# A hybrid encoder layer on one core: transfers and reciprocals of the attention mix dealt over later steps, five dense parts at the head of the out-projection, norm sums by head pair

## The chip, the cores and the metric

The kernel runs on one core of a Trainium2 chip. The core has four engines that compute: TensorE (PE, matrix products; its weight loads are shown as PEld), VectorE (DVE), ScalarE (ACT) and GpSimd (POOL); SyncE (SP) only issues transfers. Each engine runs its own instructions in order and waits for the others by semaphores. What counts is the device time in microseconds (us), the median of several runs.

## The reference, cut to what matters

One layer of an encoder, for 1024 positions of width 1024, in float32. Two mixers stand side by side: mixer A is dense attention (8 query heads on 2 key heads), mixer B a mixture of three dilated windows (8 heads). Their outputs are normed apart, go through one out-projection and are added to x; then follows a gated channel mixer of width 2816 with a convolution over three positions.

```
hn = rms_norm(x, norm1_g)
proj = hn @ w_in                       # 1024 x 2304: qA kA vA qB kB vB
out_a = global_gqa_attention(qa, ka, va)
out_b = dilated_mixture_attention(rms_norm(qb), rms_norm(kb), vb)
mixed = concat([rms_norm(out_a, outa_norm_g), rms_norm(out_b, outb_norm_g)])
x = x + mixed @ w_out
x = x + conv_ffn(rms_norm(x, norm2_g), w_up, conv_w, conv_b, w_down)
```

## The kernel before

Each float32 operand is split into a high and a low half (an ACT copy for the high, a DVE subtraction for the low), and each product is three matmuls: high by high, high by low, low by high. That is why most values pass ACT and DVE ("split") before PE may use them.

The stages follow one another on PE: some warm-up products of constants (`WARM`, L595), the projection with its norms (to some 188 us), mixer A in 16 groups (`a_main_bounded`, to 331), mixer B in 36 steps of which four make a head (`dilated`, to 458), the out-projection (`project`, to some 571), the up-projection with the convolution (`product`, to 975) and the down-projection. A scheduler of the framework orders the instructions of each engine from the order of the program and the waits. `with tc.issue_after(x)` keeps what is written under it behind instruction x on its engine: in this text, it is pinned behind x.

Both mixers make their outputs transposed, heads on partitions and positions in columns, with the softmax denominators as one more row. To divide by them, the row is written out by a transfer, comes back as a small tile, is inverted, is written out again (`rna` for A, `rnb` for B) and is read back spread over the 64 partitions of a head. For mixer A these are `recip_load` (L800), `recip` (L803, L804), `scale_load` (L811) and the multiplication `scale_a` (L814); `squares` (L817, L818) and `squares_sum` (L823, a small matmul with ones) then make the sums for the output norm. For mixer B, at the end of a head, two ACT copies (L1052, L1053) take the head's result out of PSUM, the denominators go out (L1055), `b_move` (L1060) moves the head into place, `b_recip` holds the reciprocal (L1064), the write (L1065) and the spread (L1066), and `scale_b` multiplies a pair of heads (L1070).

In mixer B a step is: scores on PE (`b_s_bounded`, L1014), exponentials on ACT (L1015), multiplication by the distance weights on DVE (`b_p_bounded`: L1023 in the coarse steps, L1027, L1029, L1030 in the fine ones) and, three steps later, the products with the values on PE (`b_pv_bounded`, L1042, L1049). Scores and results lie in PSUM banks that are used in turn, so PE's scores wait for the DVE multiplication of an earlier step. The table `dilated_late` puts the late work of mixer A into steps of mixer B, `dense_late` into groups of mixer A. The fills (L1274) write constants into tiles for mixer B.

The out-projection works in 16 parts: (i, 0) is the half of tile i (128 positions) that comes from mixer A, called dense here, (i, 1) that from mixer B. A part is two halves of 12 matmuls (`part_out`, L1187 to L1189) over six PSUM banks. `mix_split` (L1200, L1201) splits a part's input, `part_add` (L1195) scales its output by the norm and adds x (`x_part`, L1204, loads it) or the first half. Behind (i, 1) `h2_a` makes the second norm (squares L1223, tiny operations of DVE, L1233) and writes the tile out (L1234, `rscr`); `h2_b` transposes it on PE (L206) and splits it (L229 to L256), and `t_split` (L1263, L1264) and `wu_prep` (L1646 to L1656) make the sums that the up-projection takes.

All loads and stores of these stages are issued by SP, in one order. The lines that set the steps of mixer B are

```
h1, i1 = divmod(n - 8, 4)
if h1 >= 0 and i1 == 0:
    b_recip(h1)
```

so that head h's reciprocal is written in step 4h + 8 and its `b_move` in step 4h + 7; the last head's stand in `project()`, where `b_move(7)` is called once more.

Of the kernel before, what the change touches and what calls it, by code (L numbers as in the profile page):

```python
# [20 lines left out]
D = 1024  # L21
# [50 lines left out]
WARM = 10  # L72
# [22 lines left out]
F_ACS = (O_F + 6048, O_F + 6048, O_F + 2048)  # L95
# [20 lines left out]
F_XS = [O_F + o for o in (2560, 7680, 0, 1024)]  # L116
# [28 lines left out]
def tile_encoder_layer(ctx, tc, x, xT, w_in, w_kv, consts, norm2_g, w_out, w_up, convs,  # L145
# [17 lines left out]
    def emit(bounded):  # L163
# [578 lines left out]
        pairs = [1]  # L742

        def a_main_bounded(g, prep, tail, late, plan, late_plan):
# [23 lines left out]
            for j in range(4):  # L768
# [9 lines left out]
                act(f(p, 1024), bank(st, 1024), AF.Exp)  # L778
# [4 lines left out]
                vec.tensor_tensor(r(pl, 1024), f(p, 1024), rf(ph, 1024), op=OP.subtract)  # L783
# [36 lines left out]
        def squares_sum(ns, where, dst):  # L820
            b = next_tr()
            for c, n in enumerate(ns):
                mm(bank(b, 1, c), f(F_ACS[where] + 128 * (n % 2), 128), f(O_ONE, 1), start=True, stop=True)  # L823
            if where == 2:
                vec.tensor_scalar(f(dst + ns[0], len(ns)), bank(b, len(ns)), 1.0 / 512, EPS, op0=OP.mult, op1=OP.add)
            else:
                act(f(dst + ns[0], len(ns)), bank(b, len(ns)), AF.Copy, scale=1.0 / 512, bias=EPS)
# [189 lines left out]
        exps, probs = {}, [None]  # L1017
# [14 lines left out]
        def b_pv_bounded(h, i):  # L1032
# [18 lines left out]
            if i == 3:  # L1051
                act(f(F_OS, 512)[0:65], bank(6)[0:65], AF.Copy)  # L1052
                act(f(F_OS + 512, 512)[0:65], bank(7)[0:65], AF.Copy)  # L1053
# [8 lines left out]
        def b_recip(h):  # L1062
# [3 lines left out]
            dma(rf(R_RBB[h // 2 % 2], 1024)[p:p + 64], spread_row(None, rnb[h], 1024))  # L1066
# [108 lines left out]
        parts = [(0, 0), (1, 0), (2, 0), (3, 0), (0, 1), (1, 1), (4, 0), (2, 1), (5, 0), (3, 1), (6, 0), (4, 1), (7, 0), (5, 1), (6, 1), (7, 1)]  # L1175
# [15 lines left out]
        def part_add(i, u):  # L1191
            x0, o = F_XS[i % 4], (F_XS[i % 4], qab(seq(i)))[u]
            scale = f((SM_A + 16 + seq(i), SM_B + i)[u], 1)
            for hf in range(2):
                vec.scalar_tensor_tensor(f(o + 512 * hf, 512), bank(part_bank(i, u, hf)), scale, f(x0 + 512 * hf, 512),  # L1195
                                         op0=OP.mult, op1=OP.add)
# [6 lines left out]
        def x_part(i):  # L1203
            dma(f(F_XS[i % 4], 1024), perm_rows(x, seq(i), D))  # L1204

        def scale_out(i, n):
            v, rt, t = [f(SM_T + o + i, n) for o in (32, 40, 72)]
            act(rt, v, AF.Sqrt)
            newton(f(SM_B + i, n), v, rt, t)

        def hn(i):
            return F_X if i == 7 else F_HN

        def h2_a(i):
            t = SM_T + 48 + 8 * (i % 2)
            o = qab(seq(i))
            if bounded:
                part_add(i, 1)
# [904 lines left out]
```

## Time and profile before

| | |
|---|---|
| median of three runs | 1197.47 us (1195.58 to 1198.71) |
| profiled execution | 1197.74 us |
| its span, first to last instruction | 1196.0 us |
| mean granted clock of PE | 0.994 |
| DVE busy, 478 to 572 us | 77.9 of 94 us |
| DMA, share of 16 engines, 458 to 478 us | 0.74 |

The times of an execution are a little longer than its span, since starting and ending lie outside it. The profile gives busy times by engine and by group of instructions, for each wait the engine or transfer that ended it, and the clock that TensorE was granted (1.00 is full speed).

### The profile page before, as it was taken

What the parts mean: (1) busy time and instruction counts of PE and PEld (TensorE: products, weight loads), DVE (VectorE), ACT (ScalarE), POOL (GpSimd) and SP (SyncE); (2) the same over time, 40 slices, a digit from 0 to 9 for tenths busy, and PEclk for the clock granted to TensorE, in tenths of its full rate; (3) what the DMA queues carried; (4) which work ended last, traced back from release to release, by engine and by line L of the source; (5) the groups of instructions that cost most, each with busy time, mean ns of one, the idle gap of its engine ahead of it and who ended that gap; (6) DMA issues with size and microseconds to landing.
All of it is one profiled execution on the core that took longest, in us unless ns stands there. A gap on an engine that the chain in (4) does not pass through costs nothing.

```text
span 1196.0 us, 16295 instructions
## 1 busy us (share of the span) xinstructions
PE 1169.5 (98%) x5736; PEld 961.7 (80%) x5736; DVE 1018.8 (85%) x1402; ACT 659.5 (55%) x975; POOL 332.0 (28%) x238
## 2 busy tenths in 40 slices
PE   9999998999998998999999999999999999999998
PEld 8888886666678997787788888888888888888886
DVE  7869888899986885878999999999999997966673
ACT  6875737799886872636444453444444363543331
POOL 0000222510033420012465565645566413000000
PEclk9999999999998999999999999999999999999999
DMA  8556320121037777222223232332323267967962
GB/s 317 163 151 163 84 70 10 32 71 52 23 78 165 171 198 206 91 87 97 80 80 107 97 115 97 109 112 98 115 79 115 105 203 272 339 225 249 297 225 75
DMA packets 137783, 162.11 MB, mean 136 GB/s; under 512 B 55712, under 2 KB 91744, under 8 KB 137568
## 3 DMA queue, kind: packets, MB, share of 16 engines
q1 hardware_dynamic: 135552, 155.26, 41.4%
q0 software_dynamic: 2144, 5.77, 2.2%
q8 instruction: 46, 0.75, 0.3%
q14 instruction: 41, 0.34, 0.1%
HBM read 117.86 MB, written 33.91 MB: 127 GB/s over the span
## 4 chain that ended last, share of the span: by engine, by line
PE 77%; DVE 7%; DMA 6%; ACT 4%; issue 3%; POOL 2%; SPq 1%; DVEq 0%; POOLq 0%; ACTq 0%
PE ps L1689 11%; PE ps L1687 11%; PE ps L1688 11%; PE ps L1829 6%; PE ps L1830 6%; PE ps L1831 6%; PE ps L757 6%; PE ps L450 2%; PE ps L449 2%; PE ps L451 2%; PE ps L772 2%; PE ps L773 2%; PE ps L1187 2%; PE ps L1189 2%; PE ps L1188 1%
## 5 line engine op out<-in xcount | busy, mean ns | idle before, releaser
L1687 PE MATMUL ps<-bigr 128*128 128x512 f32 x616 | 240.0, 390 | 0.6 <-ACT bigr L1263 0.5
L1689 PE MATMUL ps<-bigr 128*128 128x512 f32 x616 | 239.9, 389 | 0.5 <-DVE bigr L1656 0.5
L1688 PE MATMUL ps<-bigr 128*128 128x512 f32 x616 | 239.8, 389 | 0.0
L1726 DVE SCALAR_TENSOR_TENSOR bigf<-bigf 128x768 f32<-128x768 f32 (+1 forms) x176 | 194.0, 1138 | 1.5 <-ACT bigf L1721 0.8
L1655 ACT ACTIVATE bigr<-bigf 128x512 fp32r<-128x512 f32 x154 | 92.0, 623 | 148.4 <-POOL bigf L1647 112.5
L1809 ACT ACTIVATE bigr<-bigf 128x1024 fp32r<-128x1024 f32 (+1 forms) x99 | 84.0, 869 | 115.2 <-PE ps L1831 66.6
L1687 PEld LDWEIGHTS ps<-bigr 128*128 128x128 f32 x616 | 115.6, 188 | 25.9 <-ACT bigr L1263 1.0
L1689 PEld LDWEIGHTS ps<-bigr 128*128 128x128 f32 x616 | 115.6, 188 | 24.8 <-DVE bigr L1656 0.9
L1688 PEld LDWEIGHTS ps<-bigr 128*128 128x128 f32 x616 | 115.6, 188 | 24.0
L1829 PE MATMUL ps<-bigr 128*128 128x512 f32 x308 | 119.8, 389 | 0.0
L1830 PE MATMUL ps<-bigr 128*128 128x512 f32 x308 | 119.8, 389 | 0.0
L1831 PE MATMUL ps<-bigr 128*128 128x512 f32 x308 | 119.8, 389 | 0.0
L1810 DVE TENSOR_TENSOR bigr<-bigf,bigr 128x1024 fp32r<-128x1024 f32 (+1 forms) x99 | 96.8, 998 | 26.4 <-ACT bigr L1809 22.7
L1656 DVE TENSOR_TENSOR bigr<-bigf,bigr 128x512 fp32r<-128x512 f32 x112 | 107.3, 958 | 4.1 <-ACT bigr L1655 3.8
L757 PE MATMUL ps<-bigr 128*66 128x512 f32 x384 | 99.8, 394 | 0.6 <-DVE bigr L783 0.6
L783 DVE TENSOR_TENSOR bigr<-bigf,bigr 128x1024 fp32r<-128x1024 f32 x64 | 81.5, 1280 | 7.1 <-ACT bigr L782 6.0
L449 PE MATMUL ps<-bigr 128*128 128x512 f32 x224 | 87.4, 390 | 0.0
L450 PE MATMUL ps<-bigr 128*128 128x512 f32 x224 | 87.2, 389 | 0.0
L451 PE MATMUL ps<-bigr 128*128 128x512 f32 x224 | 87.2, 389 | 0.0
L1692 DVE TENSOR_TENSOR bigf<-ps,bigf 128x512 f32<-128x512 f32 x110 | 75.1, 683 | 3.6 <-PE ps L1689 3.6
L757 PEld LDWEIGHTS ps<-bigr 128*66 128x66 f32 x384 | 51.1, 136 | 31.5 <-DVE bigr L783 1.1
L1656 POOL TENSOR_TENSOR bigr<-bigf,bigr 128x512 fp32r<-128x512 f32 x42 | 66.6, 1586 | 27.8 <-ACT bigr L1655 26.6
(226 smaller groups left out, 2376.7 us busy)
## 6 DMA issues: line engine op xcount, KB each, us to landing
bigf<-w_down SPq DMA_DIRECT2D x99, 256.0 KB
bigf<-w_up SPq DMA_DIRECT2D x44, 512.0 KB
bigf<-gscr SPq DMA_DIRECT2D x77, 256.0 KB
gscr<-bigf SPq DMA_DIRECT2D x31, 512.0 KB
bigf<-x SPq DMA_DIRECT2D x16, 512.0 KB
bigf<-w_in SPq DMA_DIRECT2D x29, 256.0 KB
bigf<-xT SPq DMA_DIRECT2D x16, 256.0 KB
bigf<-w_out SPq DMA_DIRECT2D x8, 512.0 KB
```

The lines of the kernel that those rows point to most:

```text
L449: mm(o, r(a, 128), r(w, 512), start=(k == 0 and n != 2 and (c == 1 or n != 3)), stop=False, skip_group_check=True)
L450: mm(o, r(a, 128), r(w + 512, 512), start=False, stop=False, skip_group_check=True)
L451: mm(o, r(a + 512, 128), r(w, 512), start=False, stop=(k == 3), skip_group_check=True)
L757: mm(bank(ob)[0:66], r(w, 66), r(p + 512 * u, 512), start=(kt == 0 and i == 0), stop=(kt == 7 and i == 2))
L1656: low = lambda eng: eng.tensor_tensor(rp(o + 512, [128, 4], [1, 128]), src, rfp(o, [128, 4], [1, 128]), op=OP.subtract)
L1687: mm(bank(b), wh, th, start=(k == 0 and n in (1, 5, 6, 7)), stop=False, skip_group_check=True)
L1688: mm(bank(b), wh, tl, start=False, stop=False, skip_group_check=True)
L1689: mm(bank(b), wl, th, start=False, stop=(k == 3), skip_group_check=True)
L1726: vec.scalar_tensor_tensor(f(a + o, n), f(i + d, n), w_, f(a + o, n), op0=OP.mult, op1=OP.add)
L1829: mm(o, ah, r(d, 512), start=(q == 0 and n in (1, 5, 2)), stop=False, skip_group_check=True)
L1830: mm(o, ah, r(d + 1024, 512), start=False, stop=False, skip_group_check=True)
L1831: mm(o, al, r(d, 512), start=False, stop=(q == NQ - 1), skip_group_check=True)
```

## The change

**Warm-up.** 14 products of constants stand ahead of the projection, for 10.

**Fills.** The four fills for mixer B are pinned behind the lows of later groups of mixer A. On DVE around the last additions (L463, L464 after the change) ahead of mixer A, before:

```order
L529 TENSOR_TENSOR bigf<-bigf 128x4x256
L463 TENSOR_TENSOR bigf<-ps,bigf 128x512
L1274 TENSOR_SCALAR bigr<-bigf 64x512 x3
L463 TENSOR_TENSOR bigf<-ps,bigf 128x512
L1274 TENSOR_SCALAR bigr<-bigf 64x512
L780 CAST bigr<-bigf 128x1024
```

and after the change:

```order
L530 TENSOR_TENSOR bigf<-bigf 128x4x256
L464 TENSOR_TENSOR bigf<-ps,bigf 128x512 x2
L781 CAST bigr<-bigf 128x1024
L784 TENSOR_TENSOR bigr<-bigf,bigr 128x1024 x2
L1391 SCALAR_TENSOR_TENSOR bigf<-bigr,bigf 128x1 x2
```

The four fills are gone from here, and the two additions follow one another.

**Mixer A's late work.** Its reciprocals of the second half, scale loads, multiplications and squares are put into later steps of mixer B, the scale loads two at a time, and the squares are pinned behind the exponentials.

**Mixer B's reciprocals.** `b_recip(h)` is written in step 4h + 10 and pinned behind that step's DVE work, for heads 0 to 5; head 6 stands in step 33, head 7 in `project()`. On SP, which issues the transfers, around the first denominators of mixer B (L1055; rna is the reciprocals of mixer A, rnb those of mixer B, vscr, kscr and tee are loads of later heads), before:

```order
L804 DMA rna<-bigf 128x2x16
L849 DMA bigf<-vscr 32x8x64
L843 DMA bigf<-vscr 128x8x64
L811 DMA bigr<-rna 64x512 x6
L1055 DMA bigf<-bigf 128x1x8
L1060 DMA bigf<-bigf 64x4x128 x2
L849 DMA bigf<-vscr 32x8x64 x3
L1065 DMA rnb<-bigf 128x8
```

and after the change (L1053 is L1055 of before, L805 is L804, L812 is L811, L1063 is L1065):

```order
L1053 DMA bigf<-bigf 128x1x8
L1058 DMA bigf<-bigf 64x4x128 x2
L847 DMA bigf<-vscr 32x8x64 x3
L855 DMA bigf<-tee 128x384 x2
L805 DMA rna<-bigf 128x2x16
L1063 DMA rnb<-bigf 128x8
L838 DMA bigf<-kscr 128x8x64
L812 DMA bigr<-rna 64x512 x2
L1064 DMA bigr<-rnb 64x1024
```

Head 0's denominators stand ahead of mixer A's reciprocals and of the scale loads, of which two follow and the rest come later.

On DVE, the first reciprocal of mixer B (L1064; L1023 begins an odd step, L1027 to L1030 make an even one), before:

```order
L1023 TENSOR_TENSOR bigf<-ps,bigf 128x1024
L1027 TENSOR_TENSOR bigf<-ps,bigf 128x1024
L1029 CAST bigr<-bigf 128x1024
L1030 TENSOR_TENSOR bigr<-bigf,bigr 128x1024
L1064 RECIPROCAL bigf<-bigf 128x8
L1023 TENSOR_TENSOR bigf<-ps,bigf 128x1024
```

and after the change, with the steps' L1021, L1025, L1027, L1028 for the lines above:

```order
L1025 TENSOR_TENSOR bigf<-ps,bigf 128x1024
L1027 CAST bigr<-bigf 128x1024
L1028 TENSOR_TENSOR bigr<-bigf,bigr 128x1024
L804 RECIPROCAL bigf<-bigf 128x32
L1021 TENSOR_TENSOR bigf<-ps,bigf 128x1024
L1062 RECIPROCAL bigf<-bigf 128x8
L1025 TENSOR_TENSOR bigf<-ps,bigf 128x1024
```

The reciprocal of mixer B stands one odd step's multiplication later than before; that of mixer A's second half is now its neighbour.

**Out-projection.** Five dense parts lead instead of four, the second `b_move(7)` is dropped, `b_recip(7)` comes first, and the loads of x, of the second norm's gain and of w_up are pinned behind its spread. On SP, at the end of mixer B, before:

```order
L1055 DMA bigf<-bigf 128x1x8
L1060 DMA bigf<-bigf 64x4x128 x2
L1204 DMA bigf<-x 128x1024
L1060 DMA bigf<-bigf 64x4x128 x2
L1065 DMA rnb<-bigf 128x8
L1912 DMA bigf<-norm_g 128x1024
L1204 DMA bigf<-x 128x1024
L1066 DMA bigr<-rnb 64x1024
```

and after the change:

```order
L1053 DMA bigf<-bigf 128x1x8
L1058 DMA bigf<-bigf 64x4x128 x2
L1203 DMA bigf<-x 128x1024
L1063 DMA rnb<-bigf 128x8
L1064 DMA bigr<-rnb 64x1024
L1203 DMA bigf<-x 128x1024 x3
L1964 DMA bigf<-norm_g 128x1024
```

One pair of L1060, the gain and one x load no longer stand between the last denominators and the spread (L1066, now L1064).

The sums for mixer B's output norm are made by head pair (`b_square`) and finished for all eight tiles at once (`b_scales`), instead of tile by tile. The splits of the parts are pinned behind part additions, the transposes (`h2_b`) go by a table of turns, one half behind each half of a part, eight low parts move from DVE to POOL, and three products of the up-projection stand ahead of the last tile's transposes instead of two.

```diff
-WARM = 10
+WARM = 14
...
             if bounded:
                 for fn, *a in dense_late.get(g, []):
-                    fn(*a)
+                    with tc.issue_after(last_exp[0] if fn is squares else last_low[0]):
+                        fn(*a)
...
+                if bounded:
+                    with tc.issue_after(last_low[0]):
+                        fills.pop(0)(O_IDF)
...
-                h1, i1 = divmod(n - 8, 4)
-                if h1 >= 0 and i1 == 0:
-                    b_recip(h1)
+                h1, i1 = divmod(n - 10, 4)
+                if 0 <= h1 < 6 and i1 == 0:
+                    with tc.issue_after(probs[0]):
+                        b_recip(h1)
                 if n == 33:
+                    with tc.issue_after(probs[0]):
+                        scale_b(1)
+                        b_recip(6)
                     wo_load(5)
...
-        dilated_late = {4: [(recip_load, 1)], 5: [(recip, 1), (scale_load, 4), (scale_load, 5), (scale_load, 6)], 9: [(scale_a, 4)],
...
+        dilated_late = {3: [(squares_sum, (2, 3), 0, SM_A)], 4: [(recip_load, 1)], 8: [(recip, 1)], 9: [(scale_load, 4)], 10: [(scale_load, 5)], 11: [(scale_load, 6)],
+                        13: [(scale_a, 4)], 14: [(scale_a, 5), (scale_a, 6)], 15: [(scale_load, 7)],
...
-        parts = [(0, 0), (1, 0), (2, 0), (3, 0), (0, 1), (1, 1), (4, 0), (2, 1), (5, 0), (3, 1), (6, 0), (4, 1), (7, 0), (5, 1), (6, 1), (7, 1)]
+        parts = [(0, 0), (1, 0), (2, 0), (3, 0), (4, 0), (0, 1), (1, 1), (2, 1), (5, 0), (3, 1), (4, 1), (6, 0), (5, 1), (6, 1), (7, 0), (7, 1)]
...
+        def b_square(m):
+            src, o = fp(qab(0) + 512 + 128 * m, [1024, 8], [1, 128]), F_BSQ[m > 0]
+            act(fp(o, [128, 8], [1, 128]), src, AF.Square)
+            if m:
+                vec.tensor_tensor(f(F_BSQ[0], 1024), f(F_BSQ[0], 1024), f(o, 1024), op=OP.add)
+
+        def b_scales():
+            b = next_tr()
+            v, rt, t = [f(SM_T + o, 8) for o in (32, 40, 72)]
+            for i in range(8):
+                mm(bank(b, 1, i), f(F_BSQ[0] + 128 * i, 128), f(O_ONE, 1), start=True, stop=True)
+            vec.tensor_scalar(v, bank(b, 8), 1.0 / 512, EPS, op0=OP.mult, op1=OP.add)
             act(rt, v, AF.Sqrt)
-            newton(f(SM_B + i, n), v, rt, t)
+            newton(f(SM_B, 8), v, rt, t)
...
-                (gp if i < 6 else vec).tensor_tensor(r(x0 + 1024, 512), t1, rf(x0, 512), op=OP.subtract)
+                (gp if i < 6 + bounded else vec).tensor_tensor(r(x0 + 1024, 512), t1, rf(x0, 512), op=OP.subtract)
...
-            b_move(7)
-            b_recip(7)
-            mix_split(2, 0)
-            mix_split(3, 0)
-            for k in (4, 5):
-                wo_high(k, f(F_PD[3], 1))
-                wo_low(k)
-            dma(f(F_G2, 1024), bcast(norm2_g, 1024))
+            spread_last = b_recip(7)
+            with tc.issue_after(spread_last):
+                x_part(3)
+            with tc.issue_after(copied[0]):
+                for k in (4, 5):
+                    wo_high(k)
+                    wo_low(k)
...
+            turns = {7: 0, 8: 1, 9: 2, 11: 3, 12: 4, 14: 5, 15: 6}
             for n in range(3, 16):
                 i, u = parts[n]
...
+                t = turns.get(n)
+                for half in range(2):
+                    part_out(i, u, half)
+                    if t is not None:
+                        h2_b(t, half)
+                if n == 5:
+                    b_scales()
...
+                if 5 <= n <= 13:
+                    with tc.issue_after(added):
+                        mix_split(*{5: (2, 1), 6: (5, 0), 7: (3, 1), 8: (4, 1), 9: (6, 0), 10: (5, 1), 11: (6, 1), 12: (7, 0), 13: (7, 1)}[n])
...
-            if n in (2, 4) and m > 3:
+            if n in (2, 4) and m > 3 or bounded and m < 4:
                 low(gp)
...
         product(0)
         product(1)
+        if bounded:
+            product(2)
         h2_b(7, 0)
```

More of the change, by code (lines that the diff above doesn't have):

```diff
@@ L822, in squares_sum @@
             for c, n in enumerate(ns):
[L823 to L827, printed above, removed]
+                mm(bank(b, 1, c), f(F_ACS[where] + 128 * (where != 1 and n % 2), 128), f(O_ONE, 1), start=True, stop=True)
+            act(f(dst + ns[0], len(ns)), bank(b, len(ns)), AF.Copy, scale=1.0 / 512, bias=EPS)
         def o_norm(t, step, dst, dims):
@@ L1540, in dilated @@
                         for fn, *a in dilated_late.get(n, []):
-                            fn(*a)
+                            if fn is squares:
+                                with tc.issue_after(exps[h, i]):
+                                    fn(*a)
+                            else:
+                                fn(*a)
                     if i == 0:
@@ L1915, in project @@
             part_out(2, 0, 1)
-            scale_b(3)
-            for i in range(2):
-                mix_split(i, 1)
-                squares(seq(i), 1, 2, i)
+            with tc.issue_after(copied[0]):
+                mix_split(4, 0)
+            part_add(1, 0)
             for k in (6, 7):
@@ L1987, in emit @@
             t_split(4, q, vec)
+        if bounded:
+            wu_prep(6)
         dealt, waiting = [], {}
-        for m in range(2, len(order)):
+        for m in range(2 + bounded, len(order)):
             j, n = order[m]
```

141 lines of the change are left out of this document (70 added, 71 removed).

## The prediction

> **What bounds the kernel now.** I read the page first, for the engine that sets the time; then the view of waits of PE (TensorE), for what it stands still for; then the windows around the two longest waits, for the clock; then the timelines, for what each wait hangs on.
>
> ```profile
> PE 1169.5 (98%) x5736; PEld 961.7 (80%) x5736; DVE 1018.8 (85%) x1402; ACT 659.5 (55%) x975; POOL 332.0 (28%) x238
> ```
>
> PE is busy 1169.5 of the span's 1196.0 us, and the order lists the same matmuls after the change, but for the warm-ups. So the change can gain only from the 26.5 us that PE stands idle and from stretches that it runs at a lower clock.
>
> ```profile
> PE ps L1187 <- ACT bigr L1200: 3.6, 1, 3.6
> PE ps L1014 <- DVE bigf L1023: 3.5, 1, 3.5
> PE ps L772 <- DVE bigf L463: 2.5, 2, 1.6
> PE ps L206 <- DVE bigf L1233: 2.5, 4, 1.1
> PE ps L1042 <- ACT bigf L1052: 1.7, 2, 1.1
> ...
> PE ps L823 <- ACT bigf L1246: 0.7, 1, 0.7
> ...
> PE ps L1687 <- ACT bigr L1263: 0.5, 1, 0.5
> PE ps L1689 <- DVE bigr L1656: 0.5, 1, 0.5
> ```
>
> Columns: who waits for what, then us in all, times, longest. Two single waits of 3.5 us stand out, each at a place that the change rewrites; behind each the clock falls, as the windows below show.
>
> **Part 1: reciprocals and transfers of mixer A and B.** The wait of L1014 (scores of mixer B) in the timeline around 380:
>
> ```profile
> 365.14 0.58 ACT L1053 ACTIVATE bigf<-ps 65x512 f32<-65x512 f32 x1
> ...
> 369.08 3.70 SPq L811 DMA_DIRECT2D bigr<-rna  x6
> ...
> 372.88 0.54 SPq L1055 DMA_DIRECT2D bigf<-bigf  x1
> ...
> 379.41 0.20 DVE L1064 RECIPROCAL bigf<-bigf 128x8 f32<-128x8 f32 x1 [5.67 <-DMA bigf<-bigf]
> ...
> 380.77 2.08 PE L1014 MATMUL ps<-bigr 128*128 128x256 f32 x8 [3.48 <-DVE bigf L1023]
> ...
> 383.94 1.39 PE L1042 MATMUL ps<-bigr 128*66 128x192 f32 x6 [1.09 <-ACT bigf L1052]
> ```
>
> Head 0's denominators are ready at 365.14 + 0.58 = 365.72. Their transfer (L1055) is issued at 372.88, because SP, which issues in order, first has to get rid of the six scale loads of L811 (3.70 us). So DVE stands at the reciprocal L1064 for 5.67 us, with the next L1023 queued behind it, and PE waits for that: 3.48 + 1.09 = **4.57 us**.
>
> After the change the transfer of head 0 is ahead of the scale loads on SP, which go two at a time between later ones; it can go 372.88 − 365.72 = 7.2 us earlier. That alone is more than the 5.67 us DVE stood; besides, the reciprocal comes two steps later, behind one more L1023. I take the whole 4.57 as gone. Bounds: nothing gained if the transfer still lands late (rival D); no more than 4.57. What is late next is PE itself, there being no other wait above 0.6 us in mixer B.
>
> ```profile
> 379.46:389.70 10.24, 7.83 (x39) 7.54 (x40) 8.05 (x10) 7.11 (x12) 3.55 (x2) 0.50 0.51 131
> ...
> 478.45:481.86 3.41, 3.41 (x10) 2.73 (x10) 3.41 (x5) 3.23 (x7) 0.00 (x0) 0.50 0.01 2
> ```
>
> In these windows (length, busy time of PE and others, then the granted clock) the clock is 0.50 behind both waits. Work of 7.83 us at half clock is 3.9 us at full clock, so **3.9 us** go with the first wait, and 3.41/2 = **1.7 us** with the second.
>
> **Part 2: start of the out-projection.** The second wait, at 478.19:
>
> ```profile
> 456.28 1.91 PE L1049 MATMUL ps<-bigf 128*65 128x128 f32 x16
> ...
> 459.17 0.53 SPq L1055 DMA_DIRECT2D bigf<-bigf  x1
> ...
> 460.11 0.39 PE L1187 MATMUL ps<-bigr 128*128 128x512 f32 x1
> ...
> 463.54 0.21 DVE L1120 CAST bigr<-bigf 128x1 fp32r<-128x1 f32 x2 [6.02 <-DMA bigf<-x]
> ...
> 463.96 1.28 SPq L1060 DMA_DIRECT2D bigf<-bigf  x2
> ...
> 464.88 0.39 PE L1187 MATMUL ps<-bigr 128*128 128x512 f32 x1
> ...
> 465.33 0.57 SPq L1065 DMA_DIRECT2D rnb<-bigf  x1
> ...
> 467.53 0.49 SPq L1066 DMA_DIRECT2D bigr<-rnb  x1
> ...
> 476.24 1.23 DVE L1070 TENSOR_TENSOR bigf<-bigf,bigr 128x1024 f32<-128x1024 f32 x1 [1.07 <-DMA bigr<-rnb]
> ...
> 478.19 0.59 PE L1187 MATMUL ps<-bigr 128*128 128x512 f32 x1 [3.63 <-ACT bigr L1200]
> ```
>
> The last head's denominators go out at 459.17, are turned into reciprocals only after DVE was held by L1120 (6.02 us), then written (465.33), read back spread over the partitions (467.53), used by L1070 at 476.24, split, and only then does part (0,1) start. Between the two L1187 quoted lie seven rounds of three matmuls, 4.77 us, so one is 0.227 us and a part of 24 is 5.46 us. Mixer B's last matmuls end at 456.28 + 1.91 = 458.2; the 72 matmuls of the dense parts behind them end at 458.2 + 16.4 = 474.6, where the wait begins (478.19 − 3.63).
>
> After the change a fifth dense part stands there: 96 matmuls, to 458.2 + 21.8 = 480.0. The chain to be covered: before it reached PE at 478.19, with no part of it made faster. Three of its delays also go: DVE is no longer held at L1120 (the two casts are gone), the second issue of L1060 is gone (1.28 us on SP), and the norm gain and x loads stand behind the spread. Two things are added on DVE between L1068 (the old L1070) and the split: two part additions and one sum of squares of 128x1024. By L818's 1.08 for each addition at most and L1070's 1.23 for the sum that is 2.2 to 3.4 us, some 2.7: 478.2 + 2.7 = 480.9 if nothing of the delays went, and 476 if 5 us of them go. The additions need an x whose load now starts behind the spread; by the spread's own 8.7 us (467.53 to 476.24) it is there by 476. Bounds for PE's wait: 0.9 to 0; I take 0: **−3.6**, and the half clock behind it **−1.7**.
>
> **Part 3: fills.**
>
> ```profile
> 190.35 1.62 DVE L1274 TENSOR_SCALAR bigr<-bigf 64x512 fp32r<-64x512 f32 x3
> ...
> 192.75 0.50 PE L772 MATMUL ps<-bigr 128*128 128x512 f32 x1 [1.64 <-DVE bigf L463]
> ```
>
> Three fills stand between two L463 for which PE waits; 1.62 us of them, 1.64 us of waiting. Pinned behind later steps' lows they leave: **−1.6**. In the dense mixer they lie beside matmuls; PE's longest wait there is 0.6 us, so I cost them at nothing there; without that cover the four fills at 0.54 are 2.2 us, which the bound of the new waits below holds.
>
> **Part 4: warm-ups, 10 to 14.**
>
> ```profile
> 1.18 4.63 PE L595 MATMUL ps<-bigf 128*128 128x128 f32 x20 [1.18 <-POOL bigf L593]
> 6.22 0.58 PE L311 MATMUL ps<-bigr 128*128 128x256 f32 x1 [0.41 <-ACT bigr L257]
> ...
> 9.95 0.58 PE L311 MATMUL ps<-bigr 128*128 128x256 f32 x1 [0.50 <-ACT bigr L300]
> ...
> 14.04 0.37 PE L313 MATMUL ps<-bigr 128*128 128x256 f32 x1
> 14.25 0.28 PE L311 MATMUL ps<-bigr 128*128 128x256 f32 x1
> 14.37 0.28 PE L312 MATMUL ps<-bigr 128*128 128x256 f32 x1
> ```
>
> Matmuls follow each other at 0.21 us up to 14.25 and at 0.12 from there, so the clock rises at 14.25. Eight more passes at 4.63/20 = 0.23 are 1.85 us: they end at 7.7 instead of 5.8, cover the 0.41 us of idle time and delay the first products by 7.7 − 6.2 = 1.5. If the unbroken stretch from 1.18 on lets the clock rise at 7.4 instead, the 6.8 us to 14.25 hold up to 3.4 us less; if not, 1.5 are lost. But the next products wait for ACT at 9.95 whatever PE does, which eats most of either. I take **−1.0**, bounds +1.5 and −3.4.
>
> The Trainium skill, "TensorE: Matmul & The Clock Gate", Part 1: The HAM clock gate, says that the clock is judged in free-running windows of some 3.4 us, full after one busy window and halved after an idle one. The two half-clock windows, of 3 times and once 3.41 us, agree with the window's length; by the same rule the gain of the warm-ups depends on where the windows fall at the start, and could be nought here, with the sum at 1182, inside the forecast's range.
>
> **Part 5: the rest of the out-projection.**
>
> ```profile
> 478.00:572.00 94.00, 90.11 (x420) 72.51 (x420) 77.92 (x175) 51.08 (x108) 11.63 (x8) 0.98 0.27 88
> ...
> L818 DVE TENSOR_REDUCE bigf<-bigf 128x128 f32<-128x512 f32 x8 | 8.7, 1083 | 0.0
> ...
> L1656 DVE TENSOR_TENSOR bigr<-bigf,bigr 128x512 fp32r<-128x512 f32 x5 | 4.3, 858 | 1.0 <-ACT bigr L1655 1.0
> ...
> L1251 POOL TENSOR_TENSOR bigr<-bigf,bigr 128x512 fp32r<-128x512 f32 x2 | 2.6, 1290 | 89.4 <-ACT bigr L1250 89.4
> ...
> L1251 DVE TENSOR_TENSOR bigr<-bigf,bigr 128x512 fp32r<-128x512 f32 x2 | 1.4, 677 | 0.0
> ```
>
> The first row is the window of the rest of the out-projection (94.00 us; PE, its loads, DVE, ACT, POOL), the others are groups in it. DVE, 77.92 busy, loses eight sums of 1083 ns (8.7 us) and six chains of tiny operations, and gains three additions of some 1.23; the transposes of a tile (L206) stand 36 matmuls, 8.2 us, behind the end of its part, where before some stood 24. The waits that this can shorten are those of L206, L823, L1687 and L1689 in the list of waits: 2.5 + 0.7 + 0.5 + 0.5 = 4.2. I take **−2.5**, bounds 0 and −4.2. For waits that come new, at the joints that are dealt anew (one joint sum for all tiles ahead of the first transposes, a product ahead of the last tile), I put **+2**, four at the 0.5 us of such waits in the list; bounds 0 and +6.
>
> **The sum** from the profiled execution's own 1197.74 us (its span is 1196.0; the median of the runs, 1197.47, is 0.3 below): −4.6 −3.9 −3.6 −1.7 −1.6 −1.0 −2.5 +2.0 = −16.9: **1181 us**, 1.4% faster.
>
> **The rivals.**
>
> **A, half of it comes back at part (0,1).** Against DVE's added 2.7 us the freed delays may be little; then PE waits 0.9 there, the half clock of 1.7 stays, the one chain of sums for all tiles makes the first transposes late by 2 to 3 (one operation each on PE, DVE, ACT and DVE again, with the part's own norm behind it, against 8.2 us of cover), and part 5 gains nothing (2.5): 0.9 + 1.7 + 2.5 + 2.5 = 7.6, and 1181 + 7.6 = 1189. For it: one chain now carries all eight tiles. 0.17.
>
> **B, POOL is late.** Eight low parts move from DVE to POOL, at 1290 ns for 677: 8 x 0.61 = 4.9 us in a row ahead of the first products, and 1.7 for the clock: 1188. Against it: POOL is busy for 11.63 of the 94 us only, so they may start early. 0.07. L1656 on DVE takes 858 ns, with POOL at work, where its like L1251 takes 677. The Trainium skill, "GPSIMD Engine Reference", 1. Specifications, has POOL share its memory interfaces with DVE and contend with DVE's operations of two inputs from that memory; these rows agree, and by it DVE would lose at most 0.18 us on each of some 25 such operations, 4.5 us, and the time would be 1186 if none of it were hidden.
>
> **C, slower than before.** The norm chain of a tile (two part additions, the squares, a root, a few tiny operations, L1233) grows past its 8.2 us, because DVE has splits pinned ahead of it. Each us beyond costs seven tiles one us each. It decides from 2.4 us beyond 8.2 (16.9/7): then all is given back, and at 3 us the time is 1181 + 21 = 1202. Against it: before, the worst wait behind 24 or 36 matmuls was 1.1. 0.06.
>
> **D, the order is changed but not the arrival.** The transfer of head 0 still lands at 379: 4.6 + 3.9 stay, 1189. Against it: nothing is ahead of it now that took SP's 3.7 us. 0.05.
>
> **How the numbers follow.** My forecast has 0.65, with its own range of 1175 (the bounds of parts 4 and 5 and no new waits) to 1187 (four more of new waits, part 5 at half). The range is 1174 to 1191: it takes in A, B and D and leaves out C, and what goes beyond. A measurement of this kernel can tell some 0.3% from no change, 3.6 us. Faster by more than that (below 1193.9) are the forecast, A, B and D, 0.94, less 0.09 for several of the rivals at once: 0.85; of those I put 0.08 within it and 0.01 beyond, which with C makes 0.07 for slower.
>
> **What would show it.** Right: no wait of PE near 380 and a clock of 1.0 through 379 to 390; L1187 of part (0,1) directly behind 96 others, without idle time; no 0.50 window from 470 on; no fill between the two L463 near 192; the rise of the clock before 10. Wrong: a wait of L206 above 2 us behind L1233 (A, C); of the first L1687 to L1689 behind POOL (B); DVE held at the first reciprocal by its transfer (D).

## The result, and the profile after

The changed kernel takes 1186.02 us (median of seven runs, 1184.02 to 1188.91) beside 1195.58 for the kernel before (seven runs, 1192.33 to 1198.71): a ratio of 0.9925, with a 95% interval of 0.9904 to 0.9946. That is 9.6 us or 0.8%, a little over half of the 16.9 us that were forecast. A second set of runs gave 0.9947 (0.9933 to 0.9960). The profiled execution took 1184.85, its span 1183.1. Runs more than 1.5% above the fastest of their kernel are left out of the ratios; there is one, of 1289.74 us, in last_first below.

The waits of PE in the changed kernel, from the view that the prediction opened with (who waits for what, us in all, times, longest); the lines have moved, so that L207 and L1241 here are L206 and L1233 before:

```profile
PE ps L207 <- DVE bigf L1241: 4.2, 1, 4.2
PE ps L1040 <- ACT bigf L1050: 2.0, 2, 1.3
PE ps L312 <- ACT bigr L301: 1.6, 1, 1.6
PE ps L204 <- POOL bigr L668: 1.4, 1, 1.4
...
PE ps L1720 <- ACT bigf L1729: 1.1, 1, 1.1
PE ps L1012 <- DVE bigf L1021: 0.9, 1, 0.9
...
PE ps L773 <- DVE bigf L464: 0.7, 1, 0.7
```

The two waits at the head of the old list are gone, and a new one of about their size stands there: the transposes of the last tile (L207) behind its norm (L1241). The windows of the same profile (length, busy time of PE, PEld, DVE, ACT and POOL, granted clock, DMA share, GB/s) answer to those of before:

```profile
379.46:389.70 10.24, 9.87 (x94) 9.68 (x93) 9.19 (x10) 6.24 (x10) 2.36 (x3) 1.00 1.01 210
...
554.97:558.38 3.41, 3.41 (x13) 3.01 (x14) 3.30 (x6) 2.21 (x4) 1.67 (x1) 0.50 0.13 31
```

From 379 to 390 the clock is 1.00, where it was 0.50; the one half-clock window now stands behind the new wait. The timelines of the two places that the prediction worked out, first head 0's denominators:

```profile
363.92 2.22 SPq L1053 DMA_DIRECT2D bigf<-bigf  x1
...
373.00 0.19 DVE L1062 RECIPROCAL bigf<-bigf 128x8 f32<-128x8 f32 x1
...
376.53 1.14 SPq L812 DMA_DIRECT2D bigr<-rna  x2
```

then the last head's, up to the split that part (0,1) waits for:

```profile
451.79 0.53 SPq L1053 DMA_DIRECT2D bigf<-bigf  x1
...
456.67 0.19 DVE L1062 RECIPROCAL bigf<-bigf 128x8 f32<-128x8 f32 x1
...
458.67 0.49 SPq L1064 DMA_DIRECT2D bigr<-rnb  x1
...
465.19 1.22 DVE L1068 TENSOR_TENSOR bigf<-bigf,bigr 128x1024 f32<-128x1024 f32 x1
...
468.78 1.29 DVE L1200 TENSOR_TENSOR bigr<-bigf,bigr 128x512 fp32r<-128x512 f32 x2
```

The transfer goes ahead of the scale loads, and the reciprocal waits for nothing. At the end of mixer B the multiplication L1068 ends 14.6 us behind the issue of L1053 (451.79 to 466.41), where it took 18.3 (459.17 to 477.47), and PE passes from the fifth dense part to (0,1) at 472.6 without a wait.

To see where the rest went, the idle times of PE above 0.1 us are summed here by stretch, from the PE timelines of two profiles of each kernel (the second ones are the runs before_again and after_again below); the last two rows are the lengths at half clock between the start and the end, and the spans.

| stretch, us | before | again | changed | again |
|---|---|---|---|---|
| 150 to 200, additions and fills | 3.3 | 3.4 | 1.2 | 1.6 |
| 200 to 340, mixer A | 1.4 | 1.5 | 2.4 | 3.0 |
| 340 to 420, mixer B | 5.0 | 4.8 | 0.6 | 1.0 |
| 420 to 452, its end | 1.0 | 0.9 | 3.2 | 4.0 |
| 452 to 540, out-projection | 4.1 | 2.6 | 0.0 | 0.0 |
| 540 to 600, last tiles, first products | 3.8 | 3.8 | 5.3 | 5.2 |
| half clock | 13.7 | 13.7 | 3.4 | 10.2 |
| span | 1196.0 | 1192.6 | 1183.1 | 1187.6 |

Waits of 9.3 us have gone from three stretches (the differences of the means), and 5.4 us have come in three others: 3.9 net. The half-clock lengths, of which each costs half of the work in it, went from 13.7 to 3.4 or 10.2, which is some 3.4 us more. That leaves 1.7 of the 9.0 us between the mean spans, and most of it is the start, where the clock rose only at 14.2 us in the first profile of before, which is a matter of that execution. One program has fewer or more half-clock stretches from run to run: between the two profiles of the changed kernel they make some 3.4 of the 4.5 us.

### The profile page after: what moved, and what is told of

The parts are those of the page before. It is cut to its first block, busy times and chain, and to the rows that moved or that the text cites. A ratio compares the mean times of both kernels' runs of the same rounds, so it can differ in the third digit from the quotient of the medians.

```text
span 1183.1 us, 16289 instructions
## 1 busy us (share of the span) xinstructions
PE 1162.1 (98%) x5744; PEld 957.2 (81%) x5744; DVE 1012.8 (86%) x1357; ACT 656.3 (55%) x965; POOL 345.3 (29%) x246
## 4 chain that ended last, share of the span: by engine, by line
PE 79%; DVE 9%; ACT 4%; issue 3%; DMA 2%; POOL 2%; SPq 0%; DVEq 0%; ACTq 0%; POOLq 0%
PE ps L1720 12%; PE ps L1721 12%; PE ps L1722 12%; PE ps L1864 6%; PE ps L1863 6%; PE ps L1862 6%; PE ps L450 3%; PE ps L452 3%; PE ps L451 3%; PE ps L758 3%; PE ps L1186 2%; PE ps L1185 2%; PE ps L1187 2%; DVE bigr L784 2%; PE ps L1012 1%
## 5 line engine op out<-in xcount | busy, mean ns | idle before, releaser
L1689 DVE TENSOR_TENSOR bigr<-bigf,bigr 128x512 fp32r<-128x512 f32 x108 | 102.7, 951 | 1.8 <-ACT bigr L1688 1.2
L1725 DVE TENSOR_TENSOR bigf<-ps,bigf 128x512 f32<-128x512 f32 x110 | 75.2, 683 | 8.9 <-PE ps L1722 8.8
L1689 POOL TENSOR_TENSOR bigr<-bigf,bigr 128x512 fp32r<-128x512 f32 x46 | 72.8, 1586 | 33.4 <-ACT bigr L1688 21.2
```

Of the source, the lines that this page charges most:

```text
L1689: low = lambda eng: eng.tensor_tensor(rp(o + 512, [128, 4], [1, 128]), src, rfp(o, [128, 4], [1, 128]), op=OP.subtract)
```

## The experiments

Each starts from the changed kernel unless it says otherwise. Times are medians; a ratio is to the kernel before on the same chip.

**The changed kernel again, and the kernel before again.** No edit.

> The changed kernel once more, as the mark for the others: 1186 (1184 to 1189), 0.9925 of before. If the wait of L207 on L1241 after three products (4.20 us in its first profile) is a matter of the program and not of that one execution, it is there again, at 3.5 to 5 us; if it was an accident, below 1.5.

1189.16 us (six runs), 0.9947 (0.9933 to 0.9960). The wait of L207 is there again, 4.17: a matter of the program.

> The kernel before, profiled a second time. The waits at 380 (4.6 us) and 478 (3.6 us) belong to the program and come again within 0.5 us. The rise of the clock at the start (14.2 us in its first profile) and the half-clock windows depend on the windows' place: if so, the rise may stand anywhere from 4 to 14 us.

One time, 1194.43. In its PE timeline the waits that the change removes are:

```profile
380.13 2.07 PE L1014 MATMUL ps<-bigr 128*128 128x256 f32 x8 [3.04 <-DVE bigf L1023]
383.29 2.02 PE L1042 MATMUL ps<-bigr 128*66 128x192 f32 x9 [1.09 <-ACT bigf L1052]
...
474.59 0.50 PE L1187 MATMUL ps<-bigr 128*128 128x512 f32 x1 [2.05 <-ACT bigr L1200]
```

The first pair is 4.1 for 4.6, the second wait 2.05 for 3.63: the term of 3.6 was taken from an execution on the high side, as was the whole sum (1197.74, against medians of 1193.8 to 1196.0 in four other sets of runs). The clock rose at 4.6 us, with ten warm-ups, where it had risen at 14.2.

**Ten warm-ups.** `WARM = 10`.

> 10 warm-ups for 14, nothing else. Forecast: 1.0 us slower than the changed kernel (bounds 1.5 faster and 3.4 slower); the clock rises at 10 to 14 us in the profile, where it rose at 5.4, 6.2, 6.4, 7.3 and 4.2 in five profiles with 14. Rival: the rise depends on where the clock's windows fall and not on the number: it rises at 4 to 8 here too, and the time is the same within 1 us.

1187.28 us, 0.9934 (0.9915 to 0.9954): no different from 14, though an interval of this width could hide one us. In its PE timeline the matmuls already follow each other at some 0.12 us at 7.50:

```profile
7.50 0.28 PE L314 MATMUL ps<-bigr 128*128 128x256 f32 x1
7.62 0.28 PE L312 MATMUL ps<-bigr 128*128 128x256 f32 x1
7.73 0.33 PE L313 MATMUL ps<-bigr 128*128 128x256 f32 x1
```

The trace's clock record has the rise at 6.3. So the four extra products changed nothing that can be measured. With ten the clock rose at 4.6 to 6.3 us in three profiles and at 14.2 in one, with 14 at 4.2 to 7.4 in ten; why it rose so late in that one execution isn't shown. The Trainium skill, "TensorE: Matmul & The Clock Gate", Part 1: The HAM clock gate, calls the windows free-running; the rises agree, at 14.2 and 4.6 in two executions of one kernel.

**The fills without their pin.**

```diff
-                    with tc.issue_after(last_low[0]):
-                        fills.pop(0)(O_IDF)
+                    fills.pop(0)(O_IDF)
```

> The fills without their pin, nothing else. The order puts three of them between the two L464 again: PE's waits from 150 to 200 go from 1.2 to 1.6 (three profiles of the changed kernel and its kin) to 2.6 to 3.3, by 1.6 us; time 1.6 more, which a single time cannot tell. Rival: mixer A's later groups, where the pinned fills stand, give as much back: the waits from 200 to 340 fall from 2.4 to 3.0 to 1.4 or less.

One time, 1191.17. The wait is back, 1.65 for 1.64, from the PE and DVE timeline:

```profile
188.03 1.62 DVE L1283 TENSOR_SCALAR bigr<-bigf 64x512 fp32r<-64x512 f32 x3
...
190.43 0.79 PE L773 MATMUL ps<-bigr 128*128 128x512 f32 x1 [1.65 <-DVE bigf L464]
```

Waits from 150 to 200 are 2.55, and from 200 to 340 they are 2.1, just below the 2.3 to 3.1 of the other profiles with the fills pinned: the rival, which asked for 1.4 or less, falls, but the pinned fills may cost some tenths of a us where they now stand. Behind this wait stand 6.83 us at half clock in this profile and 3.41 in before_again's, none in the first of before: the fills cost 1.65 and at times 1.7 to 3.4 more, which the prediction had left out.

**Four dense parts.** Part (4,0) goes behind (0,1), and `b_scales` behind part 4 instead of 5.

> Part (4,0) goes behind (0,1), so that four dense parts lead as before; the rest of the change stays. PE then reaches part (0,1) 5.46 us sooner, at 16.4 us behind mixer B's last matmul, where in the changed kernel's profile the first low of its input ended 18.6 us and its high 17.2 us behind it. Theory: a wait of L1185 of 0.8 to 2.2 us, too short for a half-clock window in most phases: 1187 to 1190. Rival: the queue order alone (nothing ahead of the spread) made the gain: no wait above 0.5, time 1186. Rival: the cover is worth the whole old wait: 3.6 and 1.7 for the clock, 1191.

1187.26 us, 0.9940 (0.9925 to 0.9954), no different from the changed kernel. The one wait there:

```profile
468.59 0.50 PE L1185 MATMUL ps<-bigr 128*128 128x512 f32 x1 [1.08 <-ACT bigr L1199]
```

The fifth part hides 1.1 us. The rest of the wait went with other edits of the change: the way from the issue of L1053 to the end of L1068 is 3.7 us shorter, as the numbers above show. Which of them did it was not taken apart.

**Mixer B's steps and mixer A's loads as before.** Two edits (rec_back), and then the first alone (step_back):

```diff
-                h1, i1 = divmod(n - 10, 4)
+                h1, i1 = divmod(n - 8, 4)
                 if 0 <= h1 < 6 and i1 == 0:
-                    with tc.issue_after(probs[0]):
-                        b_recip(h1)
+                    b_recip(h1)
...
-        dilated_late = {... 8: [(recip, 1)], 9: [(scale_load, 4)], 10: [(scale_load, 5)], 11: [(scale_load, 6)],
+        dilated_late = {... 5: [(recip, 1), (scale_load, 4), (scale_load, 5), (scale_load, 6)],
```

> Mixer A's second reciprocal and its three scale loads go back to step 5 of mixer B and mixer B's reciprocals to step 4h+8 without a pin. Theory: the transfer of head 0's denominators is held behind the scale loads again, DVE stands at the first reciprocal for 4 to 6 us, PE waits 3 to 5 us near 370 to 385, with a half-clock window or more behind it: 1191 to 1195. Rival: the rest of the change (buffers, later multiplications) already freed it: no wait above 1 us, 1186.

With both, the old stall returns in the timeline, 5.32 us on DVE and 3.14 on PE:

```profile
377.46 0.20 DVE L1062 RECIPROCAL bigf<-bigf 128x8 f32<-128x8 f32 x1 [5.32 <-DMA bigf<-bigf]
...
378.83 1.44 PE L1012 MATMUL ps<-bigr 128*128 128x256 f32 x8 [3.14 <-DVE bigf L1021]
```

and yet the time is 1186.75 (four runs, 0.9930, 0.9916 to 0.9944), no higher than with the change, where 1191 to 1195 was expected. Its profile has 4.7 us of waiting from 340 to 420, 3.9 more than with the change, and 2.4 from 420 to 452, against 3.2 and 4.0. Why the time shows nothing of the difference isn't known; an interval as wide as this one leaves room for some 2 us of it.

> Of rec_back only one half: mixer B's reciprocals at step 4h+8, unpinned; mixer A's reciprocal and scale loads stay dealt as changed. Theory W (a wait moved): the pin at step 4h+10 holds SP at the write of the reciprocals, with loads of later heads (L841) behind it, for which ACT and then PE wait at 425 to 441 (3.7 to 4.5 us of idle time in the two profiles, and 3.4 more of a half-clock stretch in the second); unpinned these waits fall below 2 us in all. And the wait at 380 stays away, since the scale loads are no longer ahead: below 1.5 us. Time 1181 to 1185. Rival S (steps needed): the two later steps, not the queue, removed the wait at 380; then 3 to 4.5 us of it are back near 379, as in rec_back, and the time is 1186 to 1190.

With the steps alone put back, nothing waits at 379: it is the scale loads ahead on SP that made the stall, and the later step isn't needed against it, so rival S falls. (The later step with the scale loads ahead was not tried.) But 1.6 us of waiting stand at 396, and 420 to 452 still has 2.9. 1189.09 us, 0.9943 (0.9922 to 0.9964), above the 1181 to 1185 of theory W. What stands at 425 and 438 in the changed kernel, from the timeline of its second profile:

```profile
421.58 0.46 SPq L847 DMA_DIRECT2D bigf<-vscr  x1
...
425.54 0.63 ACT L864 ACTIVATE bigr<-bigf 128x512 fp32r<-128x512 f32 x1 [1.41 <-DMA bigf<-vscr]
...
426.71 1.61 PE L1040 MATMUL ps<-bigr 128*66 128x192 f32 x15 [1.30 <-ACT bigf L1050]
...
434.76 1.15 ACT L1119 ACTIVATE bigr<-bigf 128x1024 fp32r<-128x1024 f32 x1 [4.38 <-DMA bigf<-w_out]
435.82 1.00 ACT L1013 ACTIVATE ps<-ps 128x1024 f32<-128x1024 f32 x1
436.86 1.23 DVE L1021 TENSOR_TENSOR bigf<-ps,bigf 128x1024 f32<-128x1024 f32 x1 [3.22 <-ACT ps L1013]
...
438.13 1.21 PE L1012 MATMUL ps<-bigr 128*128 128x256 f32 x8 [1.74 <-DVE bigf L1021]
```

First: ACT stands at L864 for the last of four loads L847, issued 3.96 us earlier, and PE stands for the ACT copy behind it. L864 reads the tile that `load_v` (L847) fills. Theory W named the load L841 behind the write of the reciprocals (L1063); but that one fills another tile, so this part of W is wrong. The wait at 425 is gone in step_back, but also in warm10, last_first and last_gate, which keep the later steps; in last_first L864 runs 3.11 us behind the last L847 and holds nobody up. So the step isn't shown to make this wait: it comes and goes with the landing of a load, and why that takes longer in some executions is open. Second: ACT stands 4.38 us at a copy of w_out (L1119) for its load, with an exponential (L1013) queued behind it, and so DVE and PE. In the first profile of the changed kernel this pair cost less, in the second a half-clock stretch of 6.83 us followed.

**The eight lows back on DVE.** `gp if i < 6`, `if n in (2, 4) and m > 3`, `t_split(2, q, vec)`, as in the kernel before.

> The eight low parts go back from POOL to DVE, nothing else. Theory L (lock): a DVE operation that reads two operands from SBUF stands still while POOL works, which stretched the norm chain of the last tile (operations of 0.16 us took 1.05 and 1.21); then the wait of L207 falls from 4.2 to below 1.5, the half-clock window behind it goes, DVE's L1273 (the splits) take 0.69 again, and the time is 1179 to 1183. Rival Q (queue): the chain is late because splits stand ahead of it on DVE; eight more operations of 0.68 there make it 5 us later still: wait of 4 to 9 us, time 1186 to 1192.

1187.43 us, 0.9936 (0.9923 to 0.9949): no gain that can be told, where theory L had 1179 to 1183. The wait of L207 falls to 2.83, not below 1.5, with the half-clock window still behind it: theory L is right in kind and too big in size, since POOL's sums for the products, which stay, still stretch L219 and L220 to 1.24 and 1.22 there. Rival Q, by which eight more operations on DVE make the norm later, is wrong: it was earlier. What lock means is seen in the timeline of the changed kernel, in front of the wait:

```profile
549.36 1.74 POOL L1675 TENSOR_TENSOR bigf<-bigf 128x512 f32<-128x512 f32 x1
...
550.05 1.05 DVE L219 TENSOR_TENSOR bigf<-bigf 128x1 f32<-128x1 f32 x1
...
551.70 1.80 POOL L1689 TENSOR_TENSOR bigr<-bigf,bigr 128x512 fp32r<-128x512 f32 x1 [0.61 <-ACT bigr L1688]
...
552.31 1.21 DVE L221 SCALAR_TENSOR_TENSOR bigf<-bigf 128x1 f32<-128x1 f32 x1
...
554.84 1.90 PE L207 MATMUL ps<-bigf 128*128 128x128 f32 x8 [4.20 <-DVE bigf L1241]
```

L219 and L221 work on one element in each partition and take 0.16 us or less in the seven other tiles. Here L219 ends at 551.10, where POOL's L1675 ends (549.36 + 1.74), and L221 at 553.52, where L1689 ends (553.50).

**The last tile's norm first, without and with POOL held back.** lows_dve, and the splits pinned:

```diff
+        with tc.issue_after(normed[0]):
+            for q in range(3):
+                t_split(2, q, vec)
```

(`normed[0]` is the last L1241; the other splits of this stage are pinned in the same way.) The second kernel also reads `SM_T + 59`, the root, instead of `SM_T + 61`, the first square, in the copies that hold POOL's sums.

> The eight lows on DVE as in lows_dve, and all splits of the first products' operands (t_split) pinned behind the last tile's norm, so that its chain comes first on DVE. POOL's three sums (L1677 to L1680) still start at the tile's first square. Theory Q (queue): the rest of the wait, 2.8 us in lows_dve, was splits standing between the tiny operations; the wait of L207 falls below 1 and no half-clock window follows: 1181 to 1184. Theory L (lock): with POOL at work beside the tiny operations they still take 1.2 us each instead of 0.16; one to three of them are stretched and 1 to 2.5 us of waiting stay: 1183 to 1186. If the splits come too late for products 4 to 6, a wait of L1722 on ACT's L1274 or DVE's L1275 of 2 us or more takes its place: 1187.

> As last_first, but POOL's three sums wait for the end of the last tile's norm (the copies that hold them read its root, not its first square). Theory L: no tiny operation (L218 to L221) takes over 0.2 us, the norm ends some 2 us sooner than in last_first, and the wait of L207 is below 0.5. If lock were no matter, the norm ends at the same place as in last_first, within 0.5. Price: the sums come later, and with them the operands of product 4 and on: a wait of L1722 of 0 to 3 us there. Time 1181 to 1186.

last_first: 1184.67 us (five runs), 0.9917 (0.9894 to 0.9940); the wait of L207 is 1.20 and 1.01, so the splits were the other part of it. last_gate: 1191.18, 0.9960 (0.9947 to 0.9973), slower than last_first, with no wait of L207 at all. The timeline of last_first (POOL at work) and then that of last_gate (POOL held):

```profile
545.42 1.28 POOL L1677 TENSOR_TENSOR bigf<-bigf 128x512 f32<-128x512 f32 x1 [1.53 <-issue]
...
545.92 0.80 DVE L219 TENSOR_TENSOR bigf<-bigf 128x1 f32<-128x1 f32 x1
```

```profile
546.83 0.16 DVE L219 TENSOR_TENSOR bigf<-bigf 128x1 f32<-128x1 f32 x1
...
556.05 3.51 POOL L1677 TENSOR_TENSOR bigf<-bigf 128x512 f32<-128x512 f32 x1 [5.49 <-DVE bigf L2016]
...
560.27 0.80 PE L1722 MATMUL ps<-bigr 128*128 128x512 f32 x1 [3.82 <-ACT bigr L1690]
```

The same operation takes 0.80 and 0.16 us, so POOL's work beside it is the cause. The price is the one that the expectation named: POOL's sums come late, are themselves held to 3.51 us for 1.28 by DVE's splits, and a product waits 3.82 for what hangs on them.

**The same edit in the kernel before.** Only the eight lows, from DVE to POOL.

> The kernel before with that one edit of the change: eight lows from DVE to POOL (tile 6's, two splits and four of w_up's). Theory L (lock): DVE operations that read two operands from SBUF stand still beside them; L1656, L1264 or L1233 show instances of 1.1 us or more next to POOL's, the waits of L206 and L1687 to L1689 from 555 to 600 grow from 3.8 to 5 or more: 1 to 4 us slower than before. Rival: DVE is relieved by 5.4 us and gains what it is spared: those waits fall below 3, 0 to 2 us faster.

1197.83 us (ten runs) beside 1193.79: 1.0035 (1.0021 to 1.0050), some 4 us slower. The timeline ahead of the transposes of the last two tiles:

```profile
551.71 1.81 POOL L1649 TENSOR_TENSOR bigf<-bigf 128x512 f32<-128x512 f32 x1
...
552.29 1.24 DVE L219 SCALAR_TENSOR_TENSOR bigf<-bigf 128x1 f32<-128x1 f32 x1
...
554.05 1.23 DVE L220 SCALAR_TENSOR_TENSOR bigf<-bigf 128x1 f32<-128x1 f32 x1
...
556.75 1.23 PE L206 MATMUL ps<-bigf 128*128 128x128 f32 x8 [2.14 <-DVE bigf L1233]
...
560.30 1.29 POOL L1251 TENSOR_TENSOR bigr<-bigf,bigr 128x512 fp32r<-128x512 f32 x1 [0.23 <-ACT bigr L1250]
560.61 1.00 DVE L219 SCALAR_TENSOR_TENSOR bigf<-bigf 128x1 f32<-128x1 f32 x1
...
561.56 1.30 POOL L1256 TENSOR_TENSOR bigf<-bigf 128x512 f32<-128x512 f32 x1
562.14 0.74 DVE L220 SCALAR_TENSOR_TENSOR bigf<-bigf 128x1 f32<-128x1 f32 x1
...
565.20 1.02 PE L206 MATMUL ps<-bigf 128*128 128x128 f32 x5 [1.98 <-DVE bigf L1233]
```

and the first of these two chains in the kernel before:

```profile
552.50 0.28 DVE L219 SCALAR_TENSOR_TENSOR bigf<-bigf 128x1 f32<-128x1 f32 x2
...
555.46 0.66 PE L206 MATMUL ps<-bigf 128*128 128x128 f32 x4 [0.18 <-DVE bigf L1233]
```

The tiny operations of both chains, some 0.15 us each in the kernel before, are stretched in the same way, and PE's waits from 540 to 600 grow from 3.8 to 5.3. Most of the growth is at the first of the two tiles, 2.14 for 0.18; there it is POOL's sums (L1649, L1647) that stand beside the chain, since the copies on DVE that let them start (L1981) now stand ahead of most of it, at 550.23, and in the kernel before directly behind it, at 552.89. At the last tile the moved lows (L1251, L1256) do, but the wait is 1.98 where two waits made 1.90; a half-clock window of 3.41 us follows it, as in the changed kernel. So the one edit is enough for what the stretch lost, partly by the order that it brings about. In the changed kernel, where the sums and DVE's splits stand beside the last tile's chain too, undoing it alone brought only 1.8 us of waits back.

**Both repairs together.** last_first, and the copy of w_out one exponential later:

```diff
-            wo_early = {... (7, 1): [(wo_load, 2), (wo_high, 3)], (7, 3): [(tied, 3), (wo_high, 2)],
-                        (7, 4): [(wo_load, 4)], (7, 5): [(tied, 2), (wo_load, 6)], ...}
+            wo_early = {... (7, 1): [(wo_load, 2)], (7, 3): [(wo_high, 3), (tied, 3)],
+                        (7, 4): [(wo_load, 4), (wo_high, 2)], (7, 5): [(tied, 2), (wo_load, 6)], ...}
```

> last_first, and the two copies of w_out that stood ahead of an exponential on ACT at 434 to 437 (L1119, waiting 3.6 and 4.4 us for their loads in two profiles) one exponential later. If these copies made the waits of L1012 and L1040 at 436 to 440 (1.4 + 0.7 in last_first, 1.7 + 1.0 in the changed kernel's second profile), these fall below 0.8 in all: 1182 to 1184, 2 us under last_first. Rival: the load lands as late as before and another instruction waits for it (the w_out lows on DVE, L1124, with L1025 behind them): the sum of the waits from 420 to 452 stays at 2.5 to 4, time as last_first.

1184.35 us (six runs, 1182.46 to 1185.25), 0.9922 (0.9903 to 0.9941). The waits of L1012 and L1040 at 436 to 440 are gone, so the copies had made them, and one of another product stands there, from the PE timeline:

```profile
437.71 0.50 PE L1185 MATMUL ps<-bigr 128*128 128x512 f32 x1 [0.91 <-DVE bigf L1025]
```

420 to 452 sums to 2.1, for 2.9 in last_first: the rival, by which another instruction waits instead, was right in part. By the ratios the time is that of last_first (0.9917), and the 2 us that were expected aren't seen. It beats the kernel before clearly. Of 13 runs of the changed kernel only two lie below its slowest; but they ran on other chips, and the ratios (0.9925 and 0.9947 for the changed kernel) do not tell the two apart.

## Why the prediction was right in direction and too large

The time lies in the range and on the side that was given; the forecast's sum was too large by about three quarters. Of its signs of being right, the clock from 379 to 390, the first product of part (0,1), the fills and the rise of the clock came out; the half-clock window past 470 and a wait of L206, now L207, above 2 us, which it named as a sign of being wrong, came too. Step by step:

- **The wait at 380, −4.6, and its half clock, −3.9.** Right in place and cause, and in the size of the wait: 340 to 420 fell from 4.9 to 0.8, and no half clock is left there, where one profile of before had 10.24 us of it and the other 6.83. rec_back and step_back together show that the order on SP did it. But the 8.5 us stand in the sum as won for good, and rec_back doesn't bear that out: undoing it costs no time that four runs can tell.
- **The wait at 478, −3.6, and its half clock, −1.7.** Gone, with the rival of a late part (0,1) (A). The wait was 3.63 and 2.05 in the two profiles of before, so the term was 0.8 too large in the mean. The working put the cover of the fifth part first and the freed delays second; four_dense shows it the other way round, 1.1 us for the part.
- **Fills, −1.6.** Right (1.65 in fills_free), and the half clock behind them was not counted.
- **Warm-ups, −1.0.** Not seen: no difference can be told, as the prediction's sentence on free-running windows allowed. The 14.2 us of the profile were one execution's.
- **The rest of the out-projection, −2.5.** This is the step that failed. The stretch from 540 to 600, which held nearly all of its waits, went from 3.8 to 5.3 and got a half-clock window that it didn't have: +3.2 instead of −2.5. The prediction counted what DVE is spared and took the eight lows on POOL for a rival (B, 0.07) that makes POOL late. before_pool shows that moving them costs some 4 us in the kernel before, and the stretched tiny operations (L219 to L221) how: POOL isn't late, DVE stands still beside it, beside its sums as well as the lows. Rival C (0.06) had the other part, splits ahead of the norm's chain on DVE, as last_first shows; but that came at the last tile alone, and not at seven. The row of L1656 (858 ns) was read as a slowdown of 0.18 us each; it was four operations of 0.69 and one of 1.53. That the 1186 worked out from it in rival B is the measured time is luck.
- **New waits, +2.** Too small and at other places: 2.7 us at the end of mixer B (means of 3.6 and 0.95), 1.2 from 200 to 340, and at times a half-clock stretch. At the end of mixer B they come from ACT, which stands in order at copies that wait for their loads: those of w_out, as best shows, and at times L864, whose load comes late for a reason that stays open.

By the medians, then, −9.6 instead of −16.9. The out-projection's end (5.7), the new waits (1.9), the warm-ups (1.0) and the wait at 478 (0.8) make 9.4, more than the 7.3 that miss; the half clock behind the fills, which the sum left out, goes the other way. What made the waits from 200 to 340 was not tried. One end of the working is off by itself: the terms named for 1187 give 1186.1.

## What to carry to other kernels

Where a stall is moved out of one in-order queue, list what now waits in every queue that the change deals anew: here, of 4.1 us won around 380, 2.7 came back in new waits at 425 to 444. Work handed from VectorE to GpSimd isn't free when VectorE's critical operations read two operands from SBUF; keep such work out of the time of a chain of tiny operations, by a pin on one side or a gate on the other, and look at what the gate delays. And take a profiled execution's half-clock windows and its place among the runs into account before adding up terms from it.

## What the runs showed of the hardware

GpSimd and VectorE operations with two operands in SBUF shut each other out, operation by operation. In the changed kernel's whole profile, the 53 subtractions of L1689 on DVE (two operands in SBUF) with no POOL instruction beside them take 682 ns in the mean, and the 55 with one 1210; L1725, of the same size with one operand in PSUM, takes 682 and 684. Of the 55, all but two that only touch a POOL instruction's last 0.06 us end 0.55 us behind the end of the one they met. The other way round, POOL's L1677 took 3.51 us for 1.28 beside DVE's splits in last_gate. The Trainium skill, "GPSIMD Engine Reference", 1. Specifications, states the contention for two SBUF inputs; the trace agrees, and shows that it is a wait for the other's end and not a sharing.

The clock falls to half without a whole idle window: in last_first two waits of 1.20 and 1.01 us, with 0.66 of work between them, were followed by 6.83 us at half clock; in fills_free waits of 0.90 and 1.65 by as much; in the first profile of before waits of 0.90 and 1.64 by none. The Trainium skill's rule ("TensorE: Matmul & The Clock Gate", Part 1: The HAM clock gate) asks for an idle window of some 3.4 us; the measurements decide, and here 2.2 and 2.6 us of idle time with work between were enough, in some executions.
